# Rotating 96 images by 90 degrees: the middle 64 images in 16 KB runs and 64 transposes, with 60 one-element VectorE writes added

## The chip, the cores and the metric

The kernel runs on one core of one Trainium2 chip. The metric is the device time of one execution in microseconds (us); the kernel before took 123.57 us as the median of 3 runs (123.53 to 123.58). Three engines matter here. VectorE (DVE in the profile) does all the arithmetic, which is only data movement in 32x32 blocks. SyncE (SP) and ScalarE (ACT) issue DMA transfers; each of the two has a queue of its own, and both queues are served by the same 16 DMA engines, which move data between HBM (the chip's main memory) and SBUF (128 partitions of on-chip memory).

## What is computed

```python
batch, c, h, w = 32, 3, 256, 256
x = np.random.randn(batch, c, h, w).astype(np.float32)
out = np.rot90(x, k=1, axes=(-2, -1)).astype(np.float32)
```

That is 96 independent images of 256x256 float32 (256 KB each, 25.17 MB in all). Column 255 - i of an image becomes row i of the result. Nothing is calculated: 25.17 MB are read from HBM, permuted in SBUF, and 25.17 MB are written back.

## The kernel before

The 96 images are 24 units of four images (1 MB). The list `AS` (line 25) says how many units make one step: four steps of one unit, four steps of four units (4 MB, 16 images), four steps of one unit. A step does three things: a load into the input tile `S_all` (lines 46 to 52), one or more transposes on VectorE from `S_all` to the output tile `U_all` (lines 54 to 60), and a store from `U_all` to HBM (lines 62 to 67). Each tile has 12 slots of 8 KB per partition, filled in a ring, so that each holds 12 of the 24 units, and a slot is used twice.

In a step of one unit each partition loads one contiguous run of 8 KB (eight image rows), one transpose (line 57) permutes 128x2048 elements, and each partition stores one run of 8 KB. In a step of four units each partition loads one run of 32 KB (32 image rows; neighbouring partitions hold rows of images 1 MB apart), eight transposes of 128x1024 (line 60) follow, and each partition stores four runs of 8 KB.

The order is set by the queues and the slots. SP issues all loads except the second and the fourth, which ACT issues ahead of its stores. ACT issues all stores. In a queue, transfers go in the order of issue, and an instruction that waits holds up what is behind it. A load into a slot waits until the transposes that read the slot's earlier content are done; a transpose waits for its load and, from the third big step on, until the stores that read the slot's earlier output have landed in HBM. There are also waits which come from eight DMA semaphores being shared in turn by the transfers: a transfer which takes a semaphore over waits for the transfer that had it before.

In what follows the data are six groups of 4 MB: g0 (the four small steps at the start), g1 to g4 (the four big steps), and g5 (the four small steps at the end). The buffers hold three groups each way, so g3 reuses the place of g0, g4 that of g1, g5 that of g2.

Of the kernel before, what the change touches and what calls it, by code (L numbers as in the profile page):

```python
# [1 line left out]

# [4 lines left out]


@with_exitstack
def kernel(  # L10
    ctx: ExitStack,
    tc: tile.TileContext,
    x: bass.AP,
    out: bass.AP,
):
    nc = tc.nc
    B, C, H, W = x.shape
    assert H == W == 256
    N = B * C
    P = 128  # L20
    R = 8
    F = R * W
    G = N // 4

    AS = [1] * 4 + [4] * 4 + [1] * 4
    assert sum(AS) == G
    NS = NU = 12
    fp32 = mybir.dt.float32

    xf = x.rearrange("b c h w -> (b c h w)")  # L30
    of = out.rearrange("b c h w -> (b c h w)")
    xg = xf.rearrange("(n f) -> n f", n=G)
    og = of.rearrange("(n f) -> n f", n=G)

    S_all = ctx.enter_context(tc.tile_pool(name="S", bufs=1)).tile([P, NS, F], fp32, name="S_all")
    U_all = ctx.enter_context(tc.tile_pool(name="U", bufs=1)).tile([P, NU, F], fp32, name="U_all")

    n = 0
    for i, a in enumerate(AS):
        s = n % NS  # L40
        assert s + a <= NS
        RI = R * a
        S = S_all[:, s : s + a].rearrange("p a f -> p (a f)")
        U = U_all[:, s : s + a]

        eng = nc.scalar if i in (1, 3) else nc.sync
        if a == 1:
            eng.dma_start(out=S, in_=xg[n].rearrange("(p f) -> p f", p=P))
        else:
            eng.dma_start(  # L50
                out=S, in_=xg[n : n + a].rearrange("a (qk f) -> qk a f", f=RI * W)
            )

        src = S.rearrange("p (r k q) -> p q r k", r=RI, q=R)[:, ::-1, :, ::-1]
        dst = U.rearrange("p a (q k r) -> p q r k a", q=R, r=RI)
        if a == 1:
            nc.vector.transpose(dst[:, :, :, :, 0], src)  # L57
        else:
            for q in range(R):
                nc.vector.transpose(dst[:, q], src[:, q])  # L60

        if a == 1:
            nc.scalar.dma_start(out=og[n].rearrange("(p f) -> p f", p=P), in_=U[:, 0])
        else:
            nc.scalar.dma_start(
                out=og[n : n + a].rearrange("a (p f) -> p a f", p=P), in_=U
            )
        n += a


# [1 line left out]
_INS = ['x']  # L72
_OUTS = [((32, 3, 256, 256), 'float32')]


# [23 lines left out]
```

## Time and profile before

| | us |
|---|---|
| median of 3 runs | 123.57 (123.53 to 123.58) |
| the profiled execution, its own time | 123.58 |
| span of the instructions in that execution | 121.8 |
| VectorE busy in the span | 94.3 (77%) |
| data moved | 50.33 MB, mean 413 GB/s over the span |
| first load issued | 0.72 |
| VectorE starts / ends | 8.24 / 110.65 |

The profile is of one execution. Its own time lies 1.78 us above its span; the rest is outside the instructions. The page gives the busy time of each engine, then the span in 40 equal slices with the busy share of each engine and of the DMA engines, then DMA queues, the chain of work that ended last, groups of instructions (count, total busy time, mean duration in ns, idle time before them) and DMA issues with the time from issue to landing. Times inside the span count from its start. Two VectorE instructions overlap a little: a 128x1024 transpose lasts 2,073 ns by its record, while starts without a wait between them lie 1,974 ns apart.

### The profile page before, as it was taken

What the parts mean: (1) busy time and instruction counts of PE and PEld (TensorE: products, weight loads), DVE (VectorE), ACT (ScalarE), POOL (GpSimd) and SP (SyncE); (2) the same over time, 40 slices, a digit from 0 to 9 for tenths busy, and PEclk for the clock granted to TensorE, in tenths of its full rate; (3) what the DMA queues carried; (4) which work ended last, traced back from release to release, by engine and by line L of the source; (5) the groups of instructions that cost most, each with busy time, mean ns of one, the idle gap of its engine ahead of it and who ended that gap; (6) DMA issues with size and microseconds to landing.
All of it is one profiled execution on the core that took longest, in us unless ns stands there. A gap on an engine that the chain in (4) does not pass through costs nothing.

```text
span 121.8 us, 127 instructions
## 1 busy us (share of the span) xinstructions
DVE 94.3 (77%) x40; POOL 0.2 (0%) x4
## 2 busy tenths in 40 slices
DVE  0029999779999999996039999899999999993000
POOL 0000000000000000000000000000000000000000
DMA  4999989899989998999899999999999999999995
GB/s 86 409 422 428 549 355 441 347 503 430 430 358 503 430 430 361 511 441 430 315 431 430 430 430 420 431 428 425 428 425 428 428 425 430 430 430 428 428 430 213
DMA packets 4992, 50.33 MB, mean 413 GB/s; under 512 B 384, under 2 KB 384, under 8 KB 384
## 3 DMA queue, kind: packets, MB, share of 16 engines
q10 hardware_dynamic: 3552, 27.26, 53.2%
q1 hardware_dynamic: 1440, 23.07, 45.0%
HBM read 25.17 MB, written 25.17 MB: 413 GB/s over the span
## 4 chain that ended last, share of the span: by engine, by line
DMA 54%; DVE 35%; DVEq 2%; issue 0%
DMA out_dram<-U_all 47%; DVE U_all L57 25%; DVE U_all L60 10%; DMA S_all<-in_x_dram 6%; DVEq L94 2%
## 5 line engine op out<-in xcount | busy, mean ns | idle before, releaser
L60 DVE STREAM_TRANSPOSE U_all<-S_all 128x1024 f32<-128x1024 f32 x32 | 63.6, 2073 | 8.1 <-issue 6.2
L57 DVE STREAM_TRANSPOSE U_all<-S_all 128x2048 f32<-128x2048 f32 x8 | 30.8, 3925 | 8.2 <-DMA S_all<-in_x_dram 8.2
L83 POOL MEMSET const-bfloat16-1.0<- 128x1 bf16 x1 | 0.1, 102 | 0.0
L83 POOL MEMSET const-uint8-127<- 128x1 uint8 x1 | 0.1, 102 | 0.0
L83 POOL MEMSET const-float32-1.0<- 128x1 f32 x1 | 0.1, 99 | 0.0
L83 POOL MEMSET const-float32-0.0<- 128x1 f32 x1 | 0.1, 98 | 0.2 <-issue 0.2
## 6 DMA issues: line engine op xcount, KB each, us to landing
S_all<-in_x_dram SPq DMA_DIRECT2D x4, 4096.0 KB, 24.4
out_dram<-U_all ACTq DMA_DIRECT2D x4, 4096.0 KB, 28.7
out_dram<-U_all ACTq DMA_DIRECT2D x8, 1024.0 KB, 15.1
S_all<-in_x_dram SPq DMA_DIRECT2D x6, 1024.0 KB, 9.7
S_all<-in_x_dram ACTq DMA_DIRECT2D x2, 1024.0 KB, 9.9
```

The costliest lines, as they stand in the source:

```text
L57: nc.vector.transpose(dst[:, :, :, :, 0], src)
L60: nc.vector.transpose(dst[:, q], src[:, q])
L83: nc = _bacc.Bacc("TRN2", target_bir_lowering=False, num_devices=1)
L94: with _tile.TileContext(nc) as tc:
```

## The change

The list of steps becomes six groups of 4 MB, written as `KINDS = [1, 2, 2, 2, 2, 1]`. The tiles come from two pools with three buffers each (32 KB per partition a buffer), so the memory in use is the same.

Kind 1 (g0 and g5) is what it was: four loads of 1 MB, four transposes of 128x2048, four stores of 1 MB, runs of 8 KB, with the second and the fourth load of g0 on ACT.

Kind 2 (g1 to g4, the middle 64 images) is loaded by two transfers of 2 MB instead of one of 4 MB, in runs of 16 KB per partition (16 image rows, neighbouring partitions 1 MB apart) instead of 32 KB. Sixteen transposes of 128x512 take the place of eight of 128x1024; each reads both halves. Two stores of 2 MB in runs of 16 KB (neighbouring partitions 2 MB apart) take the place of one store of 4 MB in runs of 8 KB.

Before all of it in program text, 60 memsets of VectorE write one element each to a tile `spare` of 1x1 that nothing reads. In the built program each memset waits on VectorE's own semaphore for the memset before it, and their place is this: 31 memsets, the first transpose of g0, one memset, the second transpose, one memset, the third, one memset, the fourth, 26 memsets, then the 64 transposes of g1 to g4 and the four of g5.

The semaphores fall differently too, as there are 32 transfers instead of 24. The waits that the built program has on them: the two loads of g2 wait for the third and fourth loads of g0; the first load of g3 for the first store of g0; the first load of g4 for the last store of g0; the loads of g5 for the first load of g3, the second store of g1, the first store of g2 and the first load of g4.

```diff
-    AS = [1] * 4 + [4] * 4 + [1] * 4
-    assert sum(AS) == G
-    NS = NU = 12
+    G = 16
+    KINDS = [1, 2, 2, 2, 2, 1]
+    F = G * H * W // P
...
+    in_pool = ctx.enter_context(tc.tile_pool(name="in_pool", bufs=3))
+    out_pool = ctx.enter_context(tc.tile_pool(name="out_pool", bufs=3))
+    spare = ctx.enter_context(tc.tile_pool(name="spare", bufs=1)).tile([1, 1], fp32, name="spare")
+    for i in range(60):
+        nc.vector.memset(spare, 0.0)
+
+    for g, kind in enumerate(KINDS):
+        S = in_pool.tile([P, F], fp32, name="S")
+        U = out_pool.tile([P, F], fp32, name="U")
+        if kind == 1:
+            R = 8
+            Sv = S.rearrange("p (s f) -> p s f", s=4)
+            Uv = U.rearrange("p (s f) -> p s f", s=4)
+            xv = xf[g].rearrange("(s p f) -> s p f", s=4, p=P)
+            ov = of[g].rearrange("(s p f) -> s p f", s=4, p=P)
+            for s in range(4):
+                eng = nc.scalar if g == 0 and s % 2 else nc.sync
+                eng.dma_start(out=Sv[:, s], in_=xv[s])
+            for s in range(4):
+                src = Sv[:, s].rearrange("p (r k q) -> p q r k", r=R, q=R)[:, ::-1, :, ::-1]
+                dst = Uv[:, s].rearrange("p (q k r) -> p q r k", q=R, r=R)
+                nc.vector.transpose(dst, src)
+                nc.scalar.dma_start(out=ov[s], in_=Uv[:, s])
         else:
-            eng.dma_start(
-                out=S, in_=xg[n : n + a].rearrange("a (qk f) -> qk a f", f=RI * W)
-            )
-        src = S.rearrange("p (r k q) -> p q r k", r=RI, q=R)[:, ::-1, :, ::-1]
-        dst = U.rearrange("p a (q k r) -> p q r k a", q=R, r=RI)
+            R = 16
+            Sv = S.rearrange("p (b f) -> p b f", b=2)
+            Uv = U.rearrange("p (a f) -> p a f", a=2)
+            xv = xf[g].rearrange("(b a qk f) -> b qk a f", b=2, a=2, f=F // 2)
+            ov = of[g].rearrange("(b a qk f) -> a qk b f", b=2, a=2, f=F // 2)
+            for b in range(2):
+                nc.sync.dma_start(out=Sv[:, b], in_=xv[b])
+            src = Sv.rearrange("p b (r k q) -> p q r k b", r=R, q=R)[:, ::-1, :, ::-1]
+            dst = Uv.rearrange("p a (q k r) -> p q r k a", q=R, r=R)
             for q in range(R):
                 nc.vector.transpose(dst[:, q], src[:, q])
-            nc.scalar.dma_start(
-                out=og[n : n + a].rearrange("a (p f) -> p a f", p=P), in_=U
-            )
+            for a in range(2):
+                nc.scalar.dma_start(out=ov[a], in_=Uv[:, a])
```

## The prediction

> **What bounds the kernel now.** I read the busy shares first, then the slices, then the timeline of VectorE against the landings of the stores.
>
> ```profile
> DVE 94.3 (77%) x40; POOL 0.2 (0%) x4
> DMA  4999989899989998999899999999999999999995
> GB/s 86 409 422 428 549 355 441 347 503 430 430 358 503 430 430 361 511 441 430 315 431 430 430 430 420 431 428 425 428 425 428 428 425 430 430 430 428 428 430 213
> ```
>
> VectorE has idle time; the DMA engines have none between the first load and the last store. A slice counts a packet where it starts, so 549 beside 355 is a 32 KB packet's edge and not a gap: in the packet records exactly 16 packets are under way at every moment from 2 to 120 us. The kernel is as fast as 16 DMA engines carry 50.33 MB, as long as they always have a transfer ready. Whether they have is decided by VectorE, so its timeline comes next.
>
> ```profile
> 8.24 15.44 DVE L57 STREAM_TRANSPOSE U_all<-S_all 128x2048 f32<-128x2048 f32 x4 [8.24 <-DMA S_all<-in_x_dram]
> 24.97 31.70 DVE L60 STREAM_TRANSPOSE U_all<-S_all 128x1024 f32<-128x1024 f32 x16 [1.30 <-DMA S_all<-in_x_dram]
> 62.83 15.93 DVE L60 STREAM_TRANSPOSE U_all<-S_all 128x1024 f32<-128x1024 f32 x8 [6.15 <-issue]
> 79.44 15.93 DVE L60 STREAM_TRANSPOSE U_all<-S_all 128x1024 f32<-128x1024 f32 x8 [0.69 <-DVE U_all L60]
> 95.27 15.38 DVE L57 STREAM_TRANSPOSE U_all<-S_all 128x2048 f32<-128x2048 f32 x4
> ```
>
> The columns are start, length, engine, line, and in brackets the idle time before. Two gaps are waits for stores. The releaser is misnamed, which the landings show:
>
> ```profile
> DMA to landing us min/median/max: 10.3/15.1/39.0
> ```
>
> This is of the small stores (L63). The last one of g0 was issued at 23.71, and 39.0 us later is 62.7: that is what g3's transposes waited for. One engine serves the two queues packet by packet, so beside loads in 32 KB packets a store in 8 KB packets gets about a fifth, and 1 MB of store took 12.2 us. Neither gap cost anything in the end: DMA was full all the while.
>
> How much later could VectorE be? After everything except the stores of g4 and g5 is moved, 8.39 MB are left, 19.6 us at 428 GB/s (the slices near the end). The last packet ended at 120.6, so that moment is 101.0. The first packet moves some 1.75 us after an issue (first load: issued 0.72 to 0.73, first packet near 1.76 and most by 2.3; I keep 1.8). So g4's transposes may end as late as **99.2** before DMA runs dry. They ended at 95.3: slack 3.9 us.
>
> **The change, part by part.**
>
> *DMA.* One engine's packets before: 256 of 8 KB at 309 ns (median of the records), 32 of 32 KB at 1,213 ns, 24 semaphore packets at 9 ns: 79.10 + 38.82 + 0.22 = 118.14 us. The changed kernel has 128 of 8 KB and 128 of 16 KB. No 16 KB packet is in the trace; on the line through the two sizes it takes 309 + (1,213 - 309)/3 = 610 ns. Bounds: half a 32 KB packet, 607, and two of 8 KB, 618. So 39.55 + 78.08 + 32 x 0.009 = 0.29 give 117.92 (117.5 to 118.9). The difference is -0.2 us, between -0.6 and +0.8; by its nearness to the line I take **-0.2**. Beside this the records hold 0.43 us of stretched packets (0.20 at 14 us, 0.23 at 58 us, 32 KB loads both). They may vanish, stay or double in the new pattern: -0.4 to +0.4; I take none of it, since their cause isn't in the profile.
>
> The pattern in HBM changes too: loads stay at neighbours 1 MB apart, stores get neighbours 2 MB apart. The slices that hold such loads show 428 to 430 GB/s, and so I cost it at nothing; bound from the other side by the worst pair of 2 us windows in that part, 58 to 62 us, 322 GB/s by starts: that is the packet edge above. Against it speaks the Trainium skill ("DMA: Bandwidth & Descriptors", Latency and other measured facts): copies of 16 KiB rows in HBM at a pitch of 2 MiB between partitions ran at 164 GB/s. At that rate 16.8 MB of stores would take 102 us instead of 39, some 63 us more. The trace's loads at 1 MB steps show none of it, and only two neighbours differ so here, so the row decides.
>
> *The first 31 memsets.* They lie in VectorE's idle time from 0.7 to 8.24, 7.5 us, hidden up to 243 ns each. The trace has no VectorE memset. Lower bound: GpSimd's memsets, which start 33 ns apart without waits. Upper: the two transposes' durations, 3,920 for 2,048 elements and 2,066 for 1,024, reach 212 ns at no element; with the wait for the predecessor (24 ns from a load's landing to the waiting transpose's start) 236.
>
> ```profile
> L83 POOL MEMSET const-float32-1.0<- 128x1 f32 x1 | 0.1, 99 | 0.0
> L60 DVE STREAM_TRANSPOSE U_all<-S_all 128x1024 f32<-128x1024 f32 x32 | 63.6, 2073 | 8.1 <-issue 6.2
> L57 DVE STREAM_TRANSPOSE U_all<-S_all 128x2048 f32<-128x2048 f32 x8 | 30.8, 3925 | 8.2 <-DMA S_all<-in_x_dram 8.2
> ```
>
> A memset reads nothing, but it waits; 99 + 24 is 123, and midway to 236 is about **0.18 us**. 31 of them end at 6.3. Without that cover they would cost 5.6 us of VectorE time.
>
> *The other 29.* Three stand between the transposes of g0 and 26 behind them: 29 x 0.18 = 5.2 us on VectorE (1.0 to 6.8). The four transposes end at 8.24 + 15.44 = 23.7, so g1 can start at 28.9 instead of 24.97. Its load lands by about 27: beside 8 KB stores, 16 KB packets get two thirds instead of four fifths, so from 14 us they go at 287 GB/s. Only the second and later stores of g0 are behind the three memsets, up to 0.5 us late, with loads queued to fill DMA.
>
> *The transposes.* Starts lie 3.822 us apart for 2,048 elements, 1.974 for 1,024: 1.805 ns an element and 0.126 us fixed. For 512: 0.126 + 0.924 = **1.05 us**. Bounds: half of 1.974, 0.987; and without overlap, on the durations, 212 + 927 ns = 1.14. A group costs 16.8 instead of 15.9. The rule against more, smaller instructions is the Trainium skill's ("VectorE: DVE Perf Modes", The TRN2 errata): its measured fixed term of about 150 cycles at 0.96 GHz would be 0.156 us, so by estimate 1.08 us, and the end of g4 below 1.9 us later. That stays within the slack.
>
> *The sum on VectorE.* 28.9 + 4 x 16.8 = **96.1** for the end of g4, if it never waits. It needn't: g0's 4 MB of stores, at a third of DMA and then more, land near 43 (two queues by turns), well before g3's turn at 62.5, and the 6.15 us gap goes. Loads of g2 land near 42 (needed 45.7). g3 was released when g0's transposes were done and lands near 57 (needed 62.5). g4, released at 45.7, shares evenly, lands near 77 to 78 (needed 79.3). g1's stores, issued at 45.7, share evenly and land by 67. g5's loads follow at 84 to 106, each ahead of its transpose (from 96.1 on, 3.82 apart, the last at 107.6). So 96.1 is 3.1 us inside the 99.2, and VectorE ends near 111.4 while stores queue until 120.6. The gap that goes is worth nothing, because DMA was full in it. With DMA 0.2 us shorter: 123.58 - 0.2 = **123.4 us**; the profiled execution lies 0.01 above the median, which changes nothing.
>
> **The rivals.**
>
> *VectorE becomes the bound.* If memsets and transposes together cost more than the 3.1 us of slack, DMA runs dry before g4's stores, and each further us is one us of time. It decides from 1.10 us per transpose at 0.18 per memset, or from about 0.27 per memset at 1.05. At both upper bounds g4 ends at 23.7 + 6.8 + 64 x 1.14 = 103.5, 4.3 late: 123.4 + 4.3 = 127.7. At 1.14 alone: 28.9 + 73.0 = 101.9, 2.7 late, 126.1. For it: two-element inner loops 16 KB apart, which no row shows. Against it: line 60 writes with steps of 8 KB and line 57 doesn't, at the same rate per element.
>
> *A smoother DMA stream.* Smaller packets and no stretched ones: -0.2 - 0.4 gives 123.0. For it: both stretches hang on 32 KB loads. Against: nothing says what stretched them.
>
> *The gaps are worth their 6.8 us.* VectorE's two waits vanish and the end comes earlier, 116.7. The full slices speak against it: 118 us of packets can't be packed into less.
>
> *DMA is dearer.* 16 KB at 618 ns and doubled stretches: +0.8 + 0.4, 124.8.
>
> **How the numbers follow.** About 0.2% (0.25 us) is what a measurement of this kernel can tell from no change. DMA remains the bound with the sum above: 0.60, own range 123.1 to 123.9, which falls 0.45 within 0.2% and 0.15 faster (123.32 is the border, near the forecast). VectorE the bound: 0.27, slower. Smoother stream in full: 0.05, faster. Dearer DMA: 0.07, slower. The 6.8 us: 0.01. So faster 0.21, same 0.45, slower 0.34. The range goes up to 126.1, the dear transposes alone, and down to 123.0: about 0.10 lies above and 0.05 below.
>
> **What would show it.** Right: slices full from start to end, no VectorE gap near 57 to 63, memsets under 0.24 us apart and done before the first transpose, transposes of 128x512 near 1.05 us apart, g4 done before 99. Wrong: a hole in DMA near 100 us, or a mean of the 128x512 starts over 1.10, or 16 KB packets far from 610 ns.

## The result, and the profile after

The changed kernel takes 124.02 us as the median of 6 runs (123.94 to 124.19) against 123.56 for the kernel before (123.44 to 123.7): ratio 1.0038, 95% interval 1.0025 to 1.0051. It is slower by 0.46 us, where the forecast was 0.2 us faster and "no change" the likeliest word.

The busy shares, the DMA slices and the DMA queues of the page of the changed kernel:

```profile
DVE 95.1 (78%) x132; POOL 0.2 (0%) x4
...
DMA  4999999999999999999999999999999999999993
...
q10 hardware_dynamic: 2592, 27.26, 52.5%
q1 hardware_dynamic: 2016, 23.07, 45.2%
q14 instruction: 1, 0.01, 0.0%
```

The DMA engines are full from start to end, as before. But the third queue line is new. The columns are packets, MB and share: one packet of 8 KB went through a queue called "instruction" while the kernel ran. The page of the kernel before has two queue lines and no such third one:

```profile
q10 hardware_dynamic: 3552, 27.26, 53.2%
q1 hardware_dynamic: 1440, 23.07, 45.0%
```

Two of the costly groups of the changed kernel (busy time and mean duration behind the first bar):

```profile
L72 DVE STREAM_TRANSPOSE U<-S 128x512 f32<-128x512 f32 x64 | 60.8, 1049 | 7.4 <-issue 4.3
...
L37 DVE MEMSET spare<- 1x1 f32 x60 | 3.5, 59 | 3.8 <-PEq L89 0.8
```

Its timeline of VectorE:

```profile
0.79 3.46 DVE L37 MEMSET spare<- 1x1 f32 x31 [0.79 <-PEq L89]
8.14 7.84 DVE L56 STREAM_TRANSPOSE U<-S 128x2048 f32<-128x2048 f32 x2 [3.89 <-DMA S<-in_x_dram]
...
26.92 30.40 DVE L72 STREAM_TRANSPOSE U<-S 128x512 f32<-128x512 f32 x32 [0.35 <-DMA S<-in_x_dram]
60.08 15.21 DVE L72 STREAM_TRANSPOSE U<-S 128x512 f32<-128x512 f32 x16 [2.76 <-DMA S<-in_x_dram]
79.57 15.20 DVE L72 STREAM_TRANSPOSE U<-S 128x512 f32<-128x512 f32 x16 [4.28 <-issue]
```

The first 31 writes take 3.46 us, 0.11 us each, and VectorE still waits 3.89 us for the first load: they are hidden. A 128x512 transpose costs 15.21/16 = 0.95 us. g4's transposes end at 94.8, well inside the 99.2 beyond which DMA would run dry. So VectorE didn't become the bound, and DMA never paused; yet the end came later.

The landing records show where. A transfer lands on each of the 16 DMA engines by itself. Each engine carries its own sixteenth of a transfer (8 of 128 packets of 8 KB), and one that is late stays late, since the others don't take its work: in the last five stores of the changed kernel the latest engine lands 0.69 to 0.73 us behind the median of the other fifteen, in those of the kernel before 0.18 to 0.20. For the last store (us):

| | median engine | second last | last | instruction packet |
|---|---|---|---|---|
| before | 120.79 | 120.89 | 120.98 | none |
| changed | 120.70 | 120.90 | 121.39 | at 29.12 us |

Fifteen engines end as before. One ends 0.49 us after the others, and the kernel ends with it. By the packet records the 8 KB instruction packet at 29.12 took 309 ns, and the 16 KB load packet that starts at 29.43, as it ends, took 1,148 ns instead of 611. The records don't name the engine of a packet; that these two lie on the late engine is inferred, and their 0.85 us together is more than the 0.49.

### The profile page after: what moved, and what is told of

The parts are those of the page before. It is cut to its first block, busy times and chain, and to the rows that moved or that the text cites. A ratio compares the mean times of both kernels' runs of the same rounds, so it can differ in the third digit from the quotient of the medians.

```text
span 122.2 us, 231 instructions
## 1 busy us (share of the span) xinstructions
DVE 95.1 (78%) x132; POOL 0.2 (0%) x4
## 4 chain that ended last, share of the span: by engine, by line
DMA 67%; DVE 15%; issue 10%; SPq 0%
DMA S<-in_x_dram 51%; DMA out_dram<-U 15%; DVE U L72 8%; DVE U L56 7%; SPq L51 0%; DVE spare L37 0%
## 5 line engine op out<-in xcount | busy, mean ns | idle before, releaser
L72 DVE STREAM_TRANSPOSE U<-S 128x512 f32<-128x512 f32 x64 | 60.8, 1049 | 7.4 <-issue 4.3
L56 DVE STREAM_TRANSPOSE U<-S 128x2048 f32<-128x2048 f32 x8 | 31.1, 3948 | 5.7 <-DMA S<-in_x_dram 5.7
L37 DVE MEMSET spare<- 1x1 f32 x60 | 3.5, 59 | 3.8 <-PEq L89 0.8
```

The costliest lines, as they stand in the source:

```text
L37: nc.vector.memset(spare, 0.0)
L56: nc.vector.transpose(dst, src)
```

## The experiments

Three theories. **A**: a program longer than what is loaded at the start has its next 8 KB fetched in the middle, through one DMA engine, which then ends late. **B**: the new pattern of transfers costs it; its 16 KB loads are stretched by 0.58 us per engine between 12 and 20 us. **C**: the writes hold VectorE back by 2 us at g1. Each run is compared with runs of the kernel before on the same chip. Instructions of an engine are counted with those that the page's busy line leaves out (waits and the like): VectorE has 51 in the span of the kernel before (the page's x40 are its transposes), 146 in the changed one.

### First four: fewer writes, and writes in the kernel before

The changed kernel without its writes, and with 30:

```diff
@@ e1_no_writes
-    for i in range(60):
+    for i in range(0):
@@ e2_writes_30
-    for i in range(60):
+    for i in range(30):
```

> The changed kernel without its 60 writes. Theory A (VectorE's longer program has to be fetched in the middle of the run, 8 KB through one DMA engine, and that engine ends late): no instruction packet in the span, the last transfer's 16 landings within 0.5 us (0.86 in the changed kernel), time 123.4 to 123.6, ratio to the kernel before 0.998 to 1.001. Theory B (the new pattern of transfers costs it, 0.58 us of stretched packets at 12 to 20 us): 123.9 to 124.1. Theory C (the writes hold VectorE back by 2 us at g1): 123.4 to 123.6 as in A, so the next runs must part A and C.

> The changed kernel with 30 writes, all ahead of the first transpose; VectorE's program has about 116 instructions in the span instead of 146. A: no fetch if what fits at the start is 128 or so, then 123.4 to 123.6; a step and not half of the cost. C: no write delays a transpose, 123.4 to 123.6. If each write costs in proportion: 123.7 to 123.8. B: 124.0.

Measured: 124.03 us (ratio 1.0041, 1.0028 to 1.0054) and 124.01 us (1.0043, 1.0031 to 1.0055). Neither gained anything. C is out for this kernel: no writes, the same time. A in the form expected here is wrong too, since both runs do have an instruction packet, e1_no_writes at 82.99 us and e2_writes_30 at 45.90. The queue lines of the page of e1_no_writes:

```profile
q10 hardware_dynamic: 2592, 27.26, 52.6%
q1 hardware_dynamic: 2016, 23.07, 45.2%
q14 instruction: 1, 0.01, 0.0%
```

With 87 VectorE instructions in the span it is fetched as well; what is loaded at the start is less than the 128 I had assumed. The last engine ends at 121.42 (second last 120.84) and 121.41 (120.96). B, which expected 124.0 for both, is still open.

The kernel before with 60 writes, and with 100:

```diff
+    spare = ctx.enter_context(tc.tile_pool(name="spare", bufs=1)).tile([1, 1], fp32, name="spare")
+    for i in range(60):
+        nc.vector.memset(spare, 0.0)
     n = 0
```

> The kernel before with the same 60 writes in the same places; about 111 VectorE instructions in the span, g1 some 2 us late. A: no fetch, 123.5 to 123.7. C: 123.9 to 124.1. B: 123.5 to 123.7.

> The kernel before with 100 writes; about 151 VectorE instructions in the span, g1 some 4 us late. A: an 8 KB instruction packet in the span, one engine late by 0.3 to 0.9 us, time 123.9 to 124.3. C: 4 us of VectorE, 124.0 to 124.8, without any engine late. B: 123.5 to 123.7.

Measured: 123.93 us (1.0038, 1.0025 to 1.0052) and 123.89 us (1.0039, 1.0024 to 1.0055) against 123.51. Both have an instruction packet at 28.66 us and one late engine (121.10 against 120.82; 121.15 against 120.69). B can't explain it, as the pattern of transfers is the old one. C can't either: with 100 writes g1 starts at 28.36 us, with 60 at 26.12, and the cost is the same. A expected no fetch with 60 writes and missed; C had that time right, but not the late engine. A fits with its bound moved to about the 64th instruction: in these five runs (the changed kernel's included) 57 to 72 VectorE instructions had started 1.5 us before the packet. The 1.5 us are an estimate of the way from request to packet, from the first load of the kernel before: issued at 0.72, its first packets start at 1.76 to 2.30.

### Next four: the changed pattern with and without a fetch

To try the new transfers without a fetch, VectorE needs fewer instructions in the same time. Four transposes of 128x2048 on contiguous quarters of the buffers take 15.3 us, as sixteen of 128x512 take 15.2. They put the middle 64 images out in another order; the transfers keep their sizes and addresses. The transposes of the first half of a group no longer wait for its second half, so g1 starts at 23.08 us instead of 26.92, and the transfers move in time with it.

```diff
-            src = Sv.rearrange("p b (r k q) -> p q r k b", r=R, q=R)[:, ::-1, :, ::-1]
-            dst = Uv.rearrange("p a (q k r) -> p q r k a", q=R, r=R)
-            for q in range(R):
-                nc.vector.transpose(dst[:, q], src[:, q])
+            for s in range(4):
+                src = S.rearrange("p (s r k q) -> p s q r k", s=4, r=8, q=8)[:, s]
+                dst = U.rearrange("p (s q k r) -> p s q r k", s=4, q=8, r=8)[:, s]
+                nc.vector.transpose(dst, src)
@@ four_transposes_0 alone
-    for i in range(60):
+    for i in range(0):
```

> The changed kernel without the writes, and in g1 to g4 four transposes of 128x2048 (15.3 us a group) instead of sixteen of 128x512 (15.2 us): the middle 64 images come out in another order, the transfers and VectorE's time are the same, VectorE's program is 48 instructions shorter (about 39 to 45 in the span). A (the fetch): no instruction packet in the span, the last transfer's landings within 0.5 us, 123.3 to 123.6. B (the pattern of transfers): 123.9 to 124.1, without any instruction packet.

> The same with the 60 writes, about 105 VectorE instructions in the span. A: an instruction packet near the 64th to 70th of them, one engine late, 123.8 to 124.1. B: as four_transposes_0. If both A and B cost: 0.4 above four_transposes_0.

Measured: 123.48 us without writes (0.9989, 0.9981 to 0.9998) and 124.01 us with them (1.0036, 1.0022 to 1.005), against 123.65. The queue lines of the page, first without and then with writes:

```profile
q10 hardware_dynamic: 2592, 27.26, 52.5%
q1 hardware_dynamic: 2016, 23.07, 45.5%
```

```profile
q10 hardware_dynamic: 2592, 27.26, 52.5%
q1 hardware_dynamic: 2016, 23.07, 45.3%
q14 instruction: 1, 0.01, 0.0%
```

B is out: the new pattern without a fetch is 0.17 us faster than the kernel before, not slower, though its 16 KB loads are stretched by 0.43 us per engine between 12 and 20 us here too. The last two engines end at 120.95 and 121.01 without the packet, at 120.85 and 121.40 with it. VectorE has 36 and 95 instructions in these spans. One packet goes with 0.53 us. (It starts at 28.21 us, when 45 VectorE instructions had started 1.5 us before, fewer than in the other runs: started instructions mark the place of a fetch only roughly.)

GpSimd has nothing to do in this kernel after four short memsets in the first 0.5 us, and nothing waits for it. That separates the fetch from anything on VectorE. A run with few writes was to stay below the bound:

```diff
@@ before_gpsimd_150
+    for i in range(150):
+        nc.gpsimd.memset(spare, 0.0)
@@ before_writes_5
+    for i in range(5):
+        nc.vector.memset(spare, 0.0)
```

> The kernel before with 150 one-element writes on GpSimd, which has nothing else to do and on which nothing waits; VectorE's program is as before. A, if it holds for any engine's program: an instruction packet early in the span (within 15 us), one DMA engine late at the end, 123.8 to 124.1. If the cost came from VectorE's own work or its waits: 123.4 to 123.6.

> The kernel before with 5 writes, 55 or 56 VectorE instructions in the span. A, with the fetch coming at about the 64th: no instruction packet, 123.4 to 123.6. If each write or the spare tile costs by itself: over 123.5 by some hundredths at most, so this one tells the step, with before_writes_60 on its other side.

before_gpsimd_150 took 123.82 us (1.002, 1.0009 to 1.0031) against 123.65, with an instruction packet at 10.94 us and the last engine at 121.22, the second last at 120.95. The sign and the mechanism are A's; the size, 0.17 us, is at the low edge of what was expected and less than half of that in the runs before.

before_writes_5 was a miss: 124.07 us (1.0038, 1.0024 to 1.0053) without an instruction packet in the span and without a late engine (121.08 and 121.12). Its span is as long as that of the kernel before, 121.9 us in the profiled execution, but 2.2 us lie outside the span instead of 1.8, in all its runs. So these 0.4 us are spent behind or ahead of the span.

### Last three: the edge, and the dose

```diff
@@ before_writes_1
+    for i in range(1):
+        nc.vector.memset(spare, 0.0)
@@ before_writes_20
+    for i in range(20):
+        nc.vector.memset(spare, 0.0)
@@ before_gpsimd_600
+    for i in range(600):
+        nc.gpsimd.memset(spare, 0.0)
```

> The kernel before with one write, 52 VectorE instructions in the span. With 5 writes no instruction packet came in the span, which was as long as before (121.9), yet 0.4 us more lay outside the span (2.2 instead of 1.8). If that is the same fetch, reached only behind the span since the program's end lies at the edge: one write is short of the edge, 123.4 to 123.7 with 1.8 us outside. If the spare tile or any write does it: 124.0 with 2.2 outside.

> The kernel before with 20 writes, 70 or 71 VectorE instructions in the span, all writes done before the first transpose. A: the instruction packet comes within the span, when the 60th or so instruction starts, 1 to 20 us before VectorE ends (90 to 110 us), one engine late by 0.3 to 0.9 us, 123.8 to 124.1, 1.8 outside the span. If a fetch costs only early in the stream: 123.5.

> The kernel before with 600 writes on GpSimd (0.147 us each in the run with 150, so some 88 us, done before the end). A: an 8 KB packet for every 128 instructions, five of them. If they go through the same DMA engine each time, that engine ends late five times over: 1.5 to 4 us, 125 to 127.5. If they go round the engines: 0.3 to 0.6 us, 123.8 to 124.2. If the cost isn't the fetch: as with 150 writes, 123.8, or in proportion to the writes, 124.3.

before_writes_1: 123.64 us (0.9996, 0.9986 to 1.0006), no packet, 1.8 us outside the span. The spare tile and a write as such cost nothing. before_writes_20: 124.05 us (1.0028, 1.0017 to 1.0039), 71 VectorE instructions, the packet late, at 95.98 us, with 64 of them started 1.5 us before; the last engine at 121.47, the second last at 121.20. Twenty writes, over at 3.0 us in 8.35 us of idle time, cost what sixty or a hundred cost. So the writes' time on VectorE is not what costs.

before_gpsimd_600: 126.00 us (1.0188, 1.0172 to 1.0203). Its busy shares, its DMA row and its instruction line:

```profile
DVE 94.3 (76%) x40; POOL 53.6 (43%) x604
...
DMA  4999999989998999999899999999999999999970
...
q14 instruction: 5, 0.04, 0.1%
```

Five packets, at 10.67, 29.53, 48.25, 67.10 and 85.99 us; 66, 195, 322, 451 and 580 GpSimd instructions had started 1.5 us before them. That is one packet for 128 instructions, and 8 KB over 128 is 64 bytes an instruction. VectorE executes the same 40 transposes in the same 94.3 us, and its last one ends at 112.5 us (110.65 before), well ahead of the last store's end. The DMA row ends in 70 instead of 95, and the stretches at the end show what that is (columns: stretch, its length, busy time of VectorE and of GpSimd with instruction counts, clock, DMA share, GB/s):

```profile
116.00:118.00 2.00, 0.00 (x0) 0.00 (x0) 1.00 0.97 410
118.00:120.00 2.00, 0.00 (x0) 0.00 (x0) 1.00 1.04 438
120.00:122.00 2.00, 0.00 (x0) 0.00 (x0) 1.00 0.21 86
122.00:124.00 2.00, 0.00 (x0) 0.00 (x0) 1.00 0.03 12
```

For the last two microseconds a thirtieth of the DMA engines is busy: one of 16, for about half the time (a packet counts where it starts). The last packets end 0.31 us apart, one after the other, up to 123.00. The landings of the last store are 121.01 for the second last engine and 123.33 for the last, 2.32 us late: 0.46 us a packet. In time it is (126.00 - 123.62)/5 = 0.48 us a packet. One engine alone is late, and by about five times what one packet costs: all five go through the same engine, and the delays add up. The writes themselves don't slow it: the GpSimd writes start every 147 ns up to 89 us, while behind each of the five packets one data packet is stretched, by 0.21 to 0.33 us.

The same holds of every fetch in these runs. Behind each of the 13 one data packet, a load or a store, starts as it ends and lasts 0.21 to 0.54 us longer than others of its size. At the end the last engine is 0.27 to 0.58 us behind the second last in the eight runs with one fetch, and 0.03 to 0.09 us in the four without (the kernel before, before_writes_1, before_writes_5, four_transposes_0).

## Why the prediction was wrong

**What bounds the kernel.** Right. DMA is full in every run until the last transfers drain, and the gaps of VectorE cost nothing: the 6.15 us wait went, others of 2.76 and 4.28 us came, and fifteen engines end as before.

**The DMA term.** This is the step that failed: "One engine's packets before: 256 of 8 KB ..., 32 of 32 KB ..., 24 semaphore packets", set against 128, 128 and 32. As a sum of data it was good: a 16 KB packet takes 611 ns against the 610 worked out, and the pattern without a fetch gained 0.17 us where -0.2 was forecast. But the sum left out the instruction packet, which is a term put at nothing without a reason, and it took 16 equal engines for granted. One engine carries one packet more and ends 0.49 us late (0.46 a packet in the run with five); instead of -0.2 it was +0.46. The signs in the trace of before were these: six 8 KB packets of the same queue in the 11 us ahead of the span, and 51 VectorE instructions in it. An 8 KB packet ahead of the span took 380 to 549 ns, so a bound of 0 to 0.5 us on one engine could have been set, though nothing in that trace told of the stretched packet behind a fetch. I counted the 92 added instructions in VectorE's time alone.

**The memsets.** Hidden, as forecast; 0.113 us each instead of 0.18, g1 at 26.9 instead of 28.9. What sets g1's start is its load, landed at 26.82, and not the writes: without any write g1 starts at 26.83. Worth nothing by themselves: 0, 30 and 60 of them give 124.03, 124.01 and 124.02. The same is true of the added transposes, in another way: the changed kernel is fetched without any write (87 instructions), and the kernel before is with 20 writes (71). Either part of the change alone costs the 0.4 us, and both together cost it once.

**The transposes.** 0.947 us instead of 1.05, on the safe side. g4 ended at 94.8 instead of 96.1, inside the limit of 99.2. That the two lie so near is partly luck. The sum had g1 2.0 us too late and each group 1.6 us too long, and held that VectorE needn't wait; it waited 2.76 and 4.28 us for the loads of g3 and g4, and the errors nearly cancel.

**The landings.** g1's load at 26.8 (27 forecast), g3's at 60.0 (57), g4's at 79.4 (77 to 78), the last of g5 at 108.0 (106). Each load waits for its slowest engine, and that one was up to 2.6 us behind the median of the others (the last load of g5); there was slack for it.

**The rivals.** VectorE as the bound: no. The gaps worth 6.8 us: no, the 6.15 us wait went and the end didn't come earlier. Dearer DMA: the right sign, but not by its mechanism; 16 KB packets are not dearer, and all stretched packets, the start's included, add up to 1.43 us per engine as before. So there was no smoother stream either. The pitch of 2 MB between neighbours costs nothing that can be seen: no 16 KB store packet took over 626 ns. (The low rate at 58 to 62 us that the prediction put down to the packet edge alone also holds the stretched packets that it had found there, 0.24 us per engine.)

The Trainium skill ("Runtime: NRT & Kernel Launch", Instruction fetch mechanics) says that an engine's instructions stream in by DMA while it runs, in blocks of 16 KiB (256 instructions), and that crossing a block is "mostly hidden". The runs here agree that it streams, but in packets of 8 KB, one for 128 instructions. Hidden it is for the engine that executes: the transposes around 29 us start 0.94 us apart, like those after them. For this kernel, bound by DMA, it isn't.

What stays open: the 0.4 us outside the span of before_writes_5. A fetch at the very end of the program would fit, as one write stays short of the edge and twenty are past it, but no record shows it. Until that is settled, where exactly the step lies is known only so far: no cost with 51 and 52 VectorE instructions, 0.4 us without a packet in the span with 56, a packet in the span from 71 on. Open too is which of the 16 engines carries the fetch, why the packet behind it is stretched, and why a fetch cost 0.17 us in before_gpsimd_150 and 0.4 to 0.5 elsewhere.

## What to carry to other kernels

When every DMA engine is full, each packet counts, also those that no line of the kernel issues: count an engine's instructions, and look for 8 KB fetches. Here the first came around the 64th instruction and, on GpSimd, the next after each 128 more, at 0.2 to 0.5 us each, for transposes and one-element writes alike and on an engine that had nothing else to do. The time is that of the slowest of 16 engines, so compare the landings of the last transfer engine by engine before looking for a cause in the mean. And look for lines in the page of after that the page of before does not have: the answer was in one of them.

## What was not expected of the hardware

- Instructions of an idle engine cost time: 600 one-element writes on GpSimd, which nothing waits for, made the kernel 1.9% slower.
- Five fetches went through one DMA engine and delayed it by 2.32 us.
- The data packet right behind a fetch was stretched in every run that had one, by 0.21 to 0.54 us; in the changed kernel it took 1,148 ns instead of 611.
- A one-element VectorE write that waits for the one before it takes 59 ns, and the next starts 113 ns after it.
- In the kernel before the last 32 KB load packets of g4, at 59 us, are stretched by 0.24 us per engine; with 5 writes it is 0.59, with 60 it is 0.03 and with 100 nothing. With 16 KB packets there is none of it. The cause was not looked for.
